# Four raw weight tiles of one part each in the place of two tiles of two parts

## The chip, the cores and the metric

The kernel runs on one core of a Trainium2 chip. A time is the device time of one execution in microseconds (us). The five engines of the core are named as the profile names them: PE (TensorE, matmuls and transposes; PEld are its weight loads), ACT (ScalarE), DVE (VectorE), POOL (GpSimd) and SP (SyncE, which here issues the weight and input transfers; SPq is its queue). Each engine works through its own instructions in order and waits on semaphores for the others.

## The reference

Two layers of a decoder trunk on 256 tokens of 1024 features, in float32. All weights come from device memory; each is used once.

```
def rmsnorm(x, g):  y = x * rsqrt(mean(x * x) + EPS);  return y * g
def swiglu(x, w_gate, w_up, w_down):  return (silu(x @ w_gate) * (x @ w_up)) @ w_down     # d_ff = 2752

per layer:
    h = h + 0.5 * swiglu(rmsnorm(h, ffn1_norm), ffn1 weights)
    u = rmsnorm(h, mix_norm);  z = u @ w_in                    # one projection, cut into columns:
        # mLSTM q|k (short causal convolution, SiLU), v, output gate, input and forget gates,
        # attention q, k, v, and two merge gates gm, ga
    A = sigmoid(o) * head_rmsnorm(mlstm_chunkwise(q, k, v, i, f), m_out_norm)
    B = sliding_window_attention(qknorm(q), qknorm(k), v, sinks)            # window 128
    h = h + (sigmoid(gm) * (A @ w_branch_m) + sigmoid(ga) * (B @ w_branch_a)) @ w_out
    h = h + 0.5 * swiglu(rmsnorm(h, ffn2_norm), ffn2 weights)
    h = h + sigmoid(rmsnorm(h, ple_norm) @ ple_gate_w) * (p[i] @ ple_proj_w)
return h
```

## The kernel before

The 256 tokens are two tiles of 128 (t = 0 and 1). The residual h stays on chip as two tiles of 128 tokens by 1024 features. A block (FFN, mixer, embedding gate) begins with a norm of each token tile: ACT sums squares (`sq`), DVE makes the mean (`ms`), POOL the power -1/2 (`r`), DVE the normed tile (`xn`), PE transposes it (`tp`), and ACT and DVE write the transpose in two pieces (`uT`).

Every product is made of three matmuls on split operands: a float32 value is cut into a rounded high piece (made by ACT, a cast) and the rest (made by DVE, a subtract), and high x high, high x low and low x high are summed. So each weight passes through three steps. SP loads a raw float32 tile (`raw`); ACT casts it to `wh`; DVE subtracts and writes `wl`. The unit of this is a *part*: 1024 columns over 128 partitions, 512 KB. Split parts live in a ring of eight pairs of tiles (RING = 8); a part leaves the ring when PE's last matmul on it is done. A raw tile holds two parts, 1 MB, and there are two raw tiles (RAW = 2). A raw tile is free for the next load when the subtract of its second part is done.

The order of all instructions is fixed when the kernel is built. A planner (class Clock) keeps an assumed time for each engine; every instruction that is written adds its assumed cost. `tick`, which is called between groups of matmuls, lets chains that are due (norms, transposes, splits, the tails of blocks) write their next step, and then calls `feed`, which starts the split of the next part if a ring place is free, its raw tile has arrived by the planner's time, and ACT and DVE are at most AHEAD ahead of PE. What is not due yet is forced by `need`, just before the matmuls that use it. The arrival of a raw tile is planned by `Clock.load`: after the tile is free and the loads before it are through, 2.9 us per MB, and a latency, `DMA = (1.0, 2.9)`. `prefetch` writes a load as soon as a raw tile is free, in the order of the list `pending`, which `unit`, `pair`, `halves`, `columns` and `ffn` fill when the blocks are set up.

The loads all go through SP's one queue: raw tiles (line 324), gains of the norms (`g`, line 498, broadcast to 128 partitions), and the embedding input `p` (line 720). At the start SP loads the first gain row, the two halves of h for t = 0, the first raw tile in two halves, h for t = 1, and the second raw tile. In the FFN, the gate and up products are `pg` and `pu` (the first columns and the last ones are `gu`), the down product `dn`; the mixer's projections are `kvq` (attention k, v, q), `v`, `og`, `z`, `gt`; `ya` and `ym` are the branch products, `yo` the output product. In the embedding gate, `pp` is the product of p and `pg` that of the gate; DVE multiplies them (`sg<-sg,pp`) and adds to h, once for each token tile and each half of the features.

Nearly all engine instructions are written through one helper, so they carry line 130.

Of the kernel before, what the change touches and what calls it, by code (L numbers as in the profile page):

```python
# [11 lines left out]
F32 = mybir.dt.float32  # L12
# [15 lines left out]
HU, QU = 2048, 1024  # L28
# [5 lines left out]
RAW = 2  # L34
# [15 lines left out]
class Part:  # L50


    def __init__(self, c0, k, n):
        self.c0, self.k, self.n = c0, k, n
        self.hi = self.lo = self.ready = None
        self.fresh = True
        self.rows = None


class Clock:  # L60
# [8 lines left out]
    DMA = (1.0, 2.9)  # L69
# [94 lines left out]
class Trunk:  # L164
# [127 lines left out]
    def unit(self, w, c0, n=NB):  # L292

        src = w[:, c0 : c0 + n].rearrange("(k p) n -> p k n", p=P)
        k = min(KT, HU // n)
        return sum((self.columns(src[:, i : i + k, :]) for i in range(0, KT, k)), [])
# [4 lines left out]
    def halves(self, src):  # L301

        units = [[], []]
        for h in range(2):
            for u in range(2):
                units[u] += self.load([Part(i * QU, 2, NB) for i in range(2)], *src(u, h))
        return units

    def pair_halves(self, w, c0):
        rows = lambda h: w[h * (D // 2) : (h + 1) * (D // 2), :].rearrange("(k p) n -> p k n", p=P)  # L310
        view = lambda raw: raw.rearrange("p (k n) -> p k n", k=KT // 2)
        return self.halves(lambda u, h: [(view, rows(h)[:, :, c0 + u * NB : c0 + (u + 1) * NB])])

    def prefetch(self, n=RAW, cut=False):

        while self.pending and self.raws and len(self.loaded) < n:
            parts, copies = self.pending.popleft()
            raw = self.rawp.tile([P, HU], F32, tag="raw", name=self.name("raw"))
            ready, arrivals = self.raws.popleft(), []
            for i in range(1 + cut):  # L320
                for view, src in copies:
                    k = src.shape[1]
                    ks = slice(i * k // 2, (i + 1) * k // 2) if cut else slice(0, k)
                    self.nc.sync.dma_start(view(raw)[:, ks], src[:, ks])
                arrivals.append(self.clock.load(ready, 1.0 / (1 + cut)))
            self.loaded.append((raw, deque((part, arrivals[i if cut else 0]) for i, part in enumerate(parts))))

    def feed(self, must=False):
# [4 lines left out]
        raw, parts = self.loaded[0]  # L333
        part, arrival = parts[0]
# [7 lines left out]
        parts.popleft()  # L342
        last = not parts
        if last:
            self.loaded.popleft()
# [4 lines left out]
        def chain():  # L350
            src = raw[:, part.c0 : part.c0 + w]
# [222 lines left out]
    def ffn(self, xT, wg, wu, wd, sink, first=6):  # L574
# [48 lines left out]
        def last_features(c0):  # L623

            def half(i):
                return lambda raw: raw[:, : KT * P].rearrange("p (k n) -> p k n", k=KT)[:, :, i * rest : (i + 1) * rest]
            unit = self.load([Part(0, KT, P)], *[(half(i), w[:, c0:].rearrange("(k p) n -> p k n", p=P))
                                                 for i, w in enumerate((wg, wu))])
# [11 lines left out]
        for k0 in range(0, nk - 2, 2):  # L640
            down += self.columns(wd[k0 * P : (k0 + 2) * P, :].rearrange("(k p) n -> p k n", p=P))
        down += self.load([Part(i * D, 1, D) for i in range(2)],
                          (lambda raw: raw[:, :D], wd[(nk - 2) * P : (nk - 1) * P, :]),
                          *[(lambda raw, p=p: raw[p, D:], wd[(nk - 1) * P :, :]) for p in (low, high)])
# [81 lines left out]
    def mix(self, l, xT, sink):  # L726
# [63 lines left out]
        rows = lambda g: lambda raw: raw[g * AD : (g + 1) * AD, :].rearrange("p (k n) -> p k n", k=4)  # L790
        units_a = self.halves(lambda u, h: [(rows(g), wa[g, :, h, :, half(u)]) for g in range(2)])
# [54 lines left out]
    def run(self, stages=None):  # L846
# [19 lines left out]
        with self.tc.manual_schedule(engines={EngineType.PE, EngineType.Activation, EngineType.DVE, EngineType.SP}):  # L866
# [4 lines left out]
            self.prefetch(1, True)  # L871
# [410 lines left out]
```

## Time and profile before

| | us |
|---|---|
| three runs | 1392.11, 1394.45, 1393.32 (median 1393.32) |
| the profiled execution, whole | 1395.02 |
| its span, first to last instruction | 1393.2 |
| PE busy, matmuls | 1371.4 (98%) |
| DVE busy | 862.3 (62%) |
| ACT busy | 726.7 (52%) |
| POOL busy | 55.0 (4%) |
| DMA, mean | 175 GB/s, 243.81 MB |

The page lists busy time of each engine, the chain of work that ended last, the costliest groups and the transfers. A row of the timeline has the start, the length, the engine, the program's line, the operation, what it writes and reads, and in brackets how long the engine sat idle before it and what ended that. A row of the waits has the engine and operation that waited, what it waited for, the total in us, how often, and the longest. "Issue to landing" of a transfer is from its instruction on SP to its completion.

### The profile page before, as it was taken

Reading aid. Unit: us, or ns where it says so; the run is one execution under the profiler, and the core shown is the slowest. Engines: PE = TensorE matmul, PEld = TensorE weight load, DVE = VectorE, ACT = ScalarE, POOL = GpSimd, SP = SyncE. Lnnn points to the kernel's source line nnn. Section 1 sums busy time; section 2 is a strip of 40 time slices with the busy share of each in tenths; the row PEclk is TensorE's granted clock in tenths of the full one; section 3 lists DMA queues with packets and bytes.
Section 4 is the critical chain, followed back from the end, with each engine's and each line's share of the span. In section 5 each row is a group of like instructions: output and inputs, shape, how many; then the busy total and the mean of one; then the engine's idle time right before and its main releaser. Section 6 shows DMA issues by size and latency. Waiting matters only on the chain.

```text
span 1393.2 us, 21942 instructions
## 1 busy us (share of the span) xinstructions
PE 1371.4 (98%) x9056; PEld 1236.9 (89%) x9056; DVE 862.3 (62%) x1213; ACT 726.7 (52%) x1138; POOL 55.0 (4%) x84
## 2 busy tenths in 40 slices
PE   8999999999999999999999999999999999999998
PEld 5999887899899889988779998878998998999886
DVE  5655457765886665554575554586658876555544
ACT  5555346874665454443554443477756554544433
POOL 0000012000000000000000000120000000000000
PEclk9999999999999999999999999999999999999999
DMA  6665645464545565565456566455445554655551
GB/s 209 218 210 167 228 136 196 124 149 151 168 152 182 166 212 186 169 229 182 165 164 210 172 207 208 143 164 145 135 134 192 173 160 161 227 191 170 205 181 61
DMA packets 125830, 243.81 MB, mean 175 GB/s; under 512 B 14977, under 2 KB 23841, under 8 KB 125730
## 3 DMA queue, kind: packets, MB, share of 16 engines
q1 hardware_dynamic: 125730, 242.41, 54.6%
q8 instruction: 71, 1.16, 0.4%
q14 instruction: 29, 0.24, 0.0%
HBM read 241.34 MB, written 1.05 MB: 174 GB/s over the span
## 4 chain that ended last, share of the span: by engine, by line
PE 90%; DMA 3%; DVE 3%; ACT 2%; issue 1%; POOL 0%; SPq 0%; ACTq 0%; POOLq 0%
PE dn L130 16%; PE pg L130 15%; PE pu L130 14%; PE gu L130 7%; PE z L130 7%; PE gt L130 6%; PE ya L130 4%; PE ym L130 3%; PE v L130 3%; PE og L130 3%; PE yo L130 3%; PE kvq L130 3%; PE tp L130 2%; PE sc L130 1%; DVE wl L130 1%; PE ha L130 1%
## 5 line engine op out<-in xcount | busy, mean ns | idle before, releaser
L130 DVE TENSOR_TENSOR wl<-raw,wh 128x1024 fp32r<-128x1024 f32 (+1 forms) x448 | 540.8, 1222 | 365.8 <-ACT wh L130 364.7
L130 ACT CAST wh<-raw 128x1024 fp32r<-128x1024 f32 x448 | 461.5, 1050 | 439.8 <-PE dn L130 86.9
L130 PE MATMUL dn<-wh,hid 128*128 128x512 f32 x688 | 218.4, 395 | 0.0
L130 PE MATMUL pg<-uT,wh 128*128 128x256 f32 x1088 | 194.6, 281 | 0.0
L130 PE MATMUL pu<-uT,wh 128*128 128x256 f32 x1088 | 193.6, 281 | 0.0
L130 PEld LDWEIGHTS pg<-uT,wh 128*128 128x128 f32 x1088 | 167.1, 189 | 0.2
L130 PEld LDWEIGHTS pu<-uT,wh 128*128 128x128 f32 x1088 | 166.9, 188 | 0.0
L130 PEld LDWEIGHTS dn<-wh,hid 128*128 128x128 f32 x688 | 129.3, 188 | 29.9
L130 PE MATMUL pg<-uT,wl 128*128 128x256 f32 x544 | 152.9, 281 | 0.0
L130 PE MATMUL pu<-uT,wl 128*128 128x256 f32 x544 | 152.9, 281 | 0.0
L130 PE MATMUL dn<-wl,hid 128*128 128x512 f32 x352 | 138.7, 394 | 0.0
L130 PEld LDWEIGHTS pu<-uT,wl 128*128 128x128 f32 x544 | 102.5, 188 | 0.0
L130 PEld LDWEIGHTS pg<-uT,wl 128*128 128x128 f32 x544 | 102.4, 188 | 0.0
L130 PE MATMUL gt<-uT,wh 128*128 128x256 f32 x512 | 93.2, 283 | 0.0
L130 PE MATMUL z<-uT,wh 128*128 128x256 f32 x512 | 92.1, 282 | 0.0
L130 PE MATMUL gu<-wh,uT 128*128 128x512 f32 x256 | 83.5, 402 | 1.9 <-ACT uT L130 1.9
L130 PEld LDWEIGHTS gt<-uT,wh 128*128 128x128 f32 x512 | 79.0, 188 | 1.2
L130 PEld LDWEIGHTS dn<-wl,hid 128*128 128x128 f32 x352 | 66.2, 188 | 15.3
L130 PEld LDWEIGHTS z<-uT,wh 128*128 128x128 f32 x512 | 78.7, 188 | 0.2
L130 PE MATMUL z<-uT,wl 128*128 128x256 f32 x256 | 72.0, 281 | 0.0
L130 PE MATMUL gt<-uT,wl 128*128 128x256 f32 x256 | 71.9, 281 | 0.0
L130 PE MATMUL kvq<-wh,uT 128*128 128x512 f32 x192 | 63.7, 401 | 0.0
(194 smaller groups left out, 2034.2 us busy)
## 6 DMA issues: line engine op xcount, KB each, us to landing
raw<-in_w_in_dram SPq DMA_DIRECT2D x60, 1024.0 KB, 5.1
raw<-in_ffn_w_up_dram SPq DMA_DIRECT2D x40, 1024.0 KB, 5.2
raw<-in_ffn_w_down_dram SPq DMA_DIRECT2D x40, 1024.0 KB, 5.5
raw<-in_ffn_w_gate_dram SPq DMA_DIRECT2D x39, 1024.0 KB, 5.7
raw<-in_w_branch_a_dram SPq DMA_DIRECT2D x16, 512.0 KB, 5.9
raw<-in_w_branch_m_dram SPq DMA_DIRECT2D x8, 1024.0 KB, 5.1
raw<-in_w_out_dram SPq DMA_DIRECT2D x8, 1024.0 KB, 5.1
raw<-in_ple_gate_w_dram SPq DMA_DIRECT2D x8, 1024.0 KB, 7.3
```

The costliest lines, as they stand in the source:

```text
L130: return issue(*args, **kw)
```

## The change

A raw tile now holds one part (1024 columns, 512 KB), and there are four of them; together they take the same space as before. A tile is free as soon as the subtract of its one part is done. Each part is its own transfer: SP's rows rise from 292 instructions to 513 in the whole program. The planner reckons with a latency of 2.0 us instead of 1.0, so that a part is planned to arrive 0.5 x 2.9 + 2.0 = 3.45 us after its load can start, where a pair was planned to take 2.9 + 1.0 = 3.9. The first loads are the same: the first raw tile was already loaded in two halves.

```diff
-HU, QU = 2048, 1024
+QU = 1024
...
-RAW = 2
+RAW = 4
...
-    DMA = (1.0, 2.9)
+    DMA = (2.0, 2.9)
...
-    def load(self, parts, *copies):
-
-        self.pending.append((parts, copies))
-        return parts
-
-    def columns(self, src, p=None):
+    def part(self, k, n, *copies):
+
+        self.pending.append(Part(k, n, copies))
+        return self.pending[-1]
+
+    def columns(self, src):
 
         _, k, n = src.shape
-        run = QU // n
-        view = lambda raw: raw[:, : k * n].rearrange("p (k n) -> p k n", k=k)
-        return self.load([Part(i * n, min(run, k - i), n) for i in range(0, k, run)], (view, src))
+        run = min(k, QU // n)
+        view = lambda raw: raw[:, : run * n].rearrange("p (k n) -> p k n", k=run)
+        return [self.part(run, n, (view, src[:, i : i + run, :])) for i in range(0, k, run)]
...
-    def prefetch(self, n=RAW, cut=False):
+    def prefetch(self, n=RAW):
 
         while self.pending and self.raws and len(self.loaded) < n:
-            parts, copies = self.pending.popleft()
-            raw = self.rawp.tile([P, HU], F32, tag="raw", name=self.name("raw"))
-            ready, arrivals = self.raws.popleft(), []
-            for i in range(1 + cut):
-                for view, src in copies:
-                    k = src.shape[1]
-                    ks = slice(i * k // 2, (i + 1) * k // 2) if cut else slice(0, k)
-                    self.nc.sync.dma_start(view(raw)[:, ks], src[:, ks])
-                arrivals.append(self.clock.load(ready, 1.0 / (1 + cut)))
-            self.loaded.append((raw, deque((part, arrivals[i if cut else 0]) for i, part in enumerate(parts))))
+            part = self.pending.popleft()
+            raw = self.rawp.tile([P, QU], F32, tag="raw", name=self.name("raw"))
+            for view, src in part.copies:
+                self.nc.sync.dma_start(view(raw), src)
+            self.loaded.append((raw, part, self.clock.load(self.raws.popleft(), 0.5)))
...
         self.store += 1
         ready = max(self.free.popleft(), arrival)
-        parts.popleft()
-        last = not parts
-        if last:
-            self.loaded.popleft()
+        self.loaded.popleft()
...
             part.ready = clock.done()
-            if last:
-                self.raws.append(part.ready)
-                self.prefetch()
+            self.raws.append(part.ready)
+            self.prefetch()
...
-            self.prefetch(1, True)
+            self.prefetch(2)
```

`halves`, `pair_halves`, `unit`, the last columns of the FFN and its down weights are written anew in the same sense: one part, one load.

No engine's compute instructions change in number or kind. Because the planned arrivals and the times at which raw tiles come free differ, their order does: 504 of PE's 9096 positions, 187 on ACT and 324 on DVE. Three places follow; a name like `wl_293` is a tile with its number in the program.

DVE at the start of the program, from the subtract of the second part on. `xn_3..` is the norm of t = 1, `uT_114` and `uT_115` its transposed low pieces, `wl` are splits. Before:

```order
L130 TENSOR_TENSOR wl_254<-raw_230,wh_253 128x1024
L130 SCALAR_TENSOR_TENSOR ms_288<-ss_270 128x1
L130 SCALAR_TENSOR_TENSOR xn_301<-h_89,r_289,g_224 128x512
L130 SCALAR_TENSOR_TENSOR xn_303<-h_89,r_289,g_225 128x512
L130 TENSOR_TENSOR wl_293<-raw_234,wh_292 128x1024
L130 TENSOR_TENSOR uT_114<-tp_309,uT_112 128x4x128
L130 TENSOR_TENSOR uT_115<-tp_316,uT_113 128x4x128
L130 TENSOR_TENSOR wl_299<-raw_234,wh_298 128x1024
```

Now:

```order
L130 TENSOR_TENSOR wl_259<-raw_232,wh_258 128x1024
L130 SCALAR_TENSOR_TENSOR ms_296<-ss_275 128x1
L130 TENSOR_TENSOR wl_291<-raw_235,wh_290 128x1024
L130 SCALAR_TENSOR_TENSOR xn_315<-h_89,r_297,g_224 128x512
L130 SCALAR_TENSOR_TENSOR xn_317<-h_89,r_297,g_225 128x512
L130 TENSOR_TENSOR wl_304<-raw_237,wh_303 128x1024
L130 TENSOR_TENSOR wl_310<-raw_256,wh_309 128x1024
L130 TENSOR_TENSOR uT_114<-tp_328,uT_112 128x4x128
L130 TENSOR_TENSOR uT_115<-tp_335,uT_113 128x4x128
```

The third part's subtract stands before the norm instead of behind it, and those of the fourth and fifth part stand before `uT`. On PE all six matmuls of the third part for t = 0 now come before the transposes of t = 1, where three came after them.

DVE at the end of the first layer's embedding gate, from the first `sg<-sg,pp` of t = 0 on; `h_88` is the residual of t = 0, `h_89` that of t = 1, the last `xn` the norm of t = 0 for the next layer. Before:

```order
L130 SCALAR_TENSOR_TENSOR sg_6988<-sg_6988,pp_6904 128x512
L130 SCALAR_TENSOR_TENSOR h_88<-sg_6988,h_88 128x512
L130 TENSOR_TENSOR wl_6983<-raw_6942,wh_6982 128x1024
L130 TENSOR_TENSOR wl_7007<-raw_6942,wh_7006 128x1024
L130 TENSOR_TENSOR wl_7013<-raw_6968,wh_7012 128x1024
L130 SCALAR_TENSOR_TENSOR sg_7031<-sg_7031,pp_6904 128x512
L130 SCALAR_TENSOR_TENSOR h_88<-sg_7031,h_88 128x512
L130 SCALAR_TENSOR_TENSOR ms_7037<-ss_6992 128x1
L130 SCALAR_TENSOR_TENSOR sg_7047<-sg_7047,pp_6907 128x512
L130 SCALAR_TENSOR_TENSOR h_89<-sg_7047,h_89 128x512
L130 SCALAR_TENSOR_TENSOR xn_7064<-h_88,r_7038,g_6853 128x512
```

Now:

```order
L130 TENSOR_TENSOR wl_7191<-raw_7130,wh_7190 128x1024
L130 TENSOR_TENSOR wl_7209<-raw_7166,wh_7208 128x1024
L130 SCALAR_TENSOR_TENSOR sg_7220<-sg_7220,pp_7123 128x512
L130 SCALAR_TENSOR_TENSOR h_88<-sg_7220,h_88 128x512
L130 TENSOR_TENSOR wl_7232<-raw_7178,wh_7231 128x1024
L130 SCALAR_TENSOR_TENSOR sg_7258<-sg_7258,pp_7123 128x512
L130 SCALAR_TENSOR_TENSOR h_88<-sg_7258,h_88 128x512
L130 SCALAR_TENSOR_TENSOR ms_7264<-ss_7224 128x1
L130 SCALAR_TENSOR_TENSOR sg_7274<-sg_7274,pp_7126 128x512
L130 SCALAR_TENSOR_TENSOR h_89<-sg_7274,h_89 128x512
L130 SCALAR_TENSOR_TENSOR xn_7291<-h_88,r_7265,g_7070 128x512
```

Between the two `sg` of t = 0 stands one split where there were three; two splits moved ahead of the first `sg`. On ACT likewise, one cast stands between the same two steps where there were two.

SP near the end of the first layer's second FFN: the raw tiles of the down weights, the gain of the embedding norm and `p`. Before:

```order
L324 DMA raw_6287<-in_ffn_w_down_dram 128x2x1024
L324 DMA raw_6342<-in_ffn_w_down_dram 128x2x1024
L324 DMA raw_6402<-in_ffn_w_down_dram 128x2x1024
L498 DMA g_6437<-in_ple_norm_dram 128x1024
L720 DMA p_6439<-in_p_dram 128x2x256
```

Now:

```order
L319 DMA raw_6550<-in_ffn_w_down_dram 128x1024
L319 DMA raw_6592<-in_ffn_w_down_dram 128x1024
L319 DMA raw_6620<-in_ffn_w_down_dram 128x1024
L487 DMA g_6638<-in_ple_norm_dram 128x1024
L707 DMA p_6640<-in_p_dram 128x2x256
```

`p` comes behind eleven down parts of half a megabyte each, where it came behind ten in five pairs.

In each layer's `kvq` stage one split stands ahead of the first two q norms (`qn`) on DVE, where two stood ahead of all four, and PE's first transposes of them come six matmuls earlier.

More of the change, by code (lines that the diff above doesn't have):

```diff
@@ L50, with __init__ @@
 class Part:
-    def __init__(self, c0, k, n):
-        self.c0, self.k, self.n = c0, k, n
+    def __init__(self, k, n, copies):
+        self.k, self.n, self.copies = k, n, copies
         self.hi = self.lo = self.ready = None
@@ L277, in consts @@
         mask(self.band[:, P:], 0, -1, 1)
-    def load(self, parts, *copies):
-        self.pending.append((parts, copies))
-        return parts
-    def columns(self, src, p=None):
+    def part(self, k, n, *copies):
+        self.pending.append(Part(k, n, copies))
+        return self.pending[-1]
+    def columns(self, src):
         _, k, n = src.shape
-        run = QU // n
-        view = lambda raw: raw[:, : k * n].rearrange("p (k n) -> p k n", k=k)
-        return self.load([Part(i * n, min(run, k - i), n) for i in range(0, k, run)], (view, src))
+        run = min(k, QU // n)
+        view = lambda raw: raw[:, : run * n].rearrange("p (k n) -> p k n", k=run)
+        return [self.part(run, n, (view, src[:, i : i + run, :])) for i in range(0, k, run)]
     def unit(self, w, c0, n=NB):
-        src = w[:, c0 : c0 + n].rearrange("(k p) n -> p k n", p=P)
-        k = min(KT, HU // n)
-        return sum((self.columns(src[:, i : i + k, :]) for i in range(0, KT, k)), [])
+        return self.columns(w[:, c0 : c0 + n].rearrange("(k p) n -> p k n", p=P))
     def pair(self, w, c0):
@@ L305, in halves @@
             for u in range(2):
-                units[u] += self.load([Part(i * QU, 2, NB) for i in range(2)], *src(u, h))
+                units[u] += [self.part(2, NB, *src(u, k)) for k in (4 * h, 4 * h + 2)]
         return units
     def pair_halves(self, w, c0):
-        rows = lambda h: w[h * (D // 2) : (h + 1) * (D // 2), :].rearrange("(k p) n -> p k n", p=P)
-        view = lambda raw: raw.rearrange("p (k n) -> p k n", k=KT // 2)
-        return self.halves(lambda u, h: [(view, rows(h)[:, :, c0 + u * NB : c0 + (u + 1) * NB])])
-    def prefetch(self, n=RAW, cut=False):
+        w = w.rearrange("(k p) n -> p k n", p=P)
+        view = lambda raw: raw.rearrange("p (k n) -> p k n", k=2)
+        return self.halves(lambda u, k: [(view, w[:, k : k + 2, c0 + u * NB : c0 + (u + 1) * NB])])
+    def prefetch(self, n=RAW):
         while self.pending and self.raws and len(self.loaded) < n:
-            parts, copies = self.pending.popleft()
-            raw = self.rawp.tile([P, HU], F32, tag="raw", name=self.name("raw"))
-            ready, arrivals = self.raws.popleft(), []
-            for i in range(1 + cut):
-                for view, src in copies:
-                    k = src.shape[1]
-                    ks = slice(i * k // 2, (i + 1) * k // 2) if cut else slice(0, k)
-                    self.nc.sync.dma_start(view(raw)[:, ks], src[:, ks])
-                arrivals.append(self.clock.load(ready, 1.0 / (1 + cut)))
-            self.loaded.append((raw, deque((part, arrivals[i if cut else 0]) for i, part in enumerate(parts))))
+            part = self.pending.popleft()
[3 more added lines that the diff above has]
+            self.loaded.append((raw, part, self.clock.load(self.raws.popleft(), 0.5)))
     def feed(self, must=False):
@@ L332, in feed @@
             return
-        raw, parts = self.loaded[0]
-        part, arrival = parts[0]
+        raw, part, arrival = self.loaded[0]
         slack = AHEAD[self.store >= STORE]
@@ L350, in chain @@
         def chain():
-            src = raw[:, part.c0 : part.c0 + w]
+            src = raw[:, :w]
             if part.rows is None:
@@ L626, in half @@
                 return lambda raw: raw[:, : KT * P].rearrange("p (k n) -> p k n", k=KT)[:, :, i * rest : (i + 1) * rest]
-            unit = self.load([Part(0, KT, P)], *[(half(i), w[:, c0:].rearrange("(k p) n -> p k n", p=P))
-                                                 for i, w in enumerate((wg, wu))])
+            unit = [self.part(KT, P, *[(half(i), w[:, c0:].rearrange("(k p) n -> p k n", p=P))
+                                       for i, w in enumerate((wg, wu))])]
             def run():
@@ L639, in ffn @@
         down = []
[L640 to L644, printed above, removed]
+        for k in range(nk - 1):
+            down.append(self.part(1, D, (lambda raw: raw, wd[k * P : (k + 1) * P, :])))
+        down.append(self.part(1, D, *[(lambda raw, p=p: raw[p], wd[(nk - 1) * P :, :]) for p in (low, high)]))
         down[-1].rows = low
@@ L789, in mix @@
         wa = a["w_branch_a"][l].rearrange("(b g j d) n -> g d b j n", b=2, g=2, j=4)
-        rows = lambda g: lambda raw: raw[g * AD : (g + 1) * AD, :].rearrange("p (k n) -> p k n", k=4)
-        units_a = self.halves(lambda u, h: [(rows(g), wa[g, :, h, :, half(u)]) for g in range(2)])
+        rows = lambda g: lambda raw: raw[g * AD : (g + 1) * AD, :].rearrange("p (k n) -> p k n", k=2)
+        units_a = self.halves(lambda u, k: [(rows(g), wa[g, :, k // 4, k % 4 : k % 4 + 2, half(u)]) for g in range(2)])
         def use_a(k, ps):
```

## The prediction

> **What bounds the kernel now.** I read the page first (busy times, the chain that ended last), then the span, then the waits of each engine (engine and what it waited for: us in total, times, longest).
>
> ```profile
> PE 1371.4 (98%) x9056; PEld 1236.9 (89%) x9056; DVE 862.3 (62%) x1213; ACT 726.7 (52%) x1138; POOL 55.0 (4%) x84
> ...
> PE 90%; DMA 3%; DVE 3%; ACT 2%; issue 1%; POOL 0%; SPq 0%; ACTq 0%; POOLq 0%
> ```
>
> ```profile
> core 0: 1393.2 us, clock 0.997
> ```
>
> TensorE (PE) works 98% of the span and holds 90% of the chain that ended last; the mean granted clock is 0.997. All that can be won without touching the matmuls is PE's idle time, 1393.2 - 1371.4 = 21.8 us, plus what a lowered clock costs. PE's waits say who holds it:
>
> ```profile
> PE tp L130 <- DVE xn L130: 3.9, 2, 2.6
> PE ya L130 <- DVE qT L130: 2.7, 2, 1.3
> ...
> PE gu L130 <- DVE wl L130: 1.5, 2, 0.8
> ```
>
> Split weights hold PE directly twice, 1.5 us. The other engines do wait for raw weights:
>
> ```profile
> ACT wh L130 <- DMA raw<-in_ffn_w_down_dram: 56.6, 24, 6.2
> ...
> SPq L324 <- DVE wl L130: 1016.9, 208, 15.2
> ```
>
> ACT waits long for arrivals, and the DMA queue (SPq) stands 1016.9 us behind the subtracts that free raw buffers. The ring of eight split tiles hides nearly all of it. So the change can act only at a few places where a norm or transpose that PE needs stands behind a split in an in-order queue, or a small load behind a big one.
>
> **The steady stages: 0.** The rows are windows (start:end and length, busy us of PE, PEld, DVE, ACT and POOL, granted clock, DMA share, GB/s), then groups and DMA issues of the page.
>
> ```profile
> 40.00:400.00 360.00, 357.72 (x2428) 323.63 (x2427) 230.02 (x350) 203.40 (x353) 17.94 (x24) 1.00 0.56 175
> ...
> 15.09:18.50 3.41, 2.75 (x16) 2.04 (x15) 1.75 (x2) 0.77 (x2) 0.00 (x0) 1.00 0.84 291
> ```
>
> ```profile
> L130 DVE TENSOR_TENSOR wl<-raw,wh 128x1024 fp32r<-128x1024 f32 (+1 forms) x448 | 540.8, 1222 | 365.8 <-ACT wh L130 364.7
> L130 ACT CAST wh<-raw 128x1024 fp32r<-128x1024 f32 x448 | 461.5, 1050 | 439.8 <-PE dn L130 86.9
> ...
> raw<-in_ffn_w_gate_dram SPq DMA_DIRECT2D x39, 1024.0 KB, 5.7
> ...
> raw<-in_ffn_w_gate_dram SPq DMA_DIRECT2D x6, 512.0 KB, 4.0
> ```
>
> In the long window PE is busy 357.72 of 360 us and the DMA engines 0.56. PE uses 448 parts in 1393 us, one per 3.1 us. Before, a raw buffer is bound for 5.7 + 1.05 + 2 x 1.22 = 9.2 us per two parts; with two buffers, 2.3 us per part. After, 4.0 + 1.05 + 1.22 = 6.3 us per part with four buffers, 1.6 us. If the four share the 291 GB/s of the fastest stretch, 0.52 MB takes 1.8 us, four 7.2 us, a buffer's cycle 9.5 us, and a part 2.4 us: still under 3.1. Both versions supply more than PE takes, so I cost the added overlap at nothing; the ring hides it. SP's issues about double, 221 more, each 0.37 us in the rows at 675.67 and 1295.71 below, take 82 us, inside its 1016.9 us of waiting. The same arithmetic instructions run.
>
> The Trainium skill, "DMA: Bandwidth & Descriptors", section "Bandwidth", speaks against the change: it asks for at least 1 MiB per DMA. The rows agree that a small transfer is dear (half the bytes, 4.0 of 5.7 us); by the rule the stages would turn DMA-bound only if transfers did not overlap, which is a rival below.
>
> **From the embedding gate to the next layer's FFN, near 675 to 699: -2.0.**
>
> ```profile
> 674.53 0.34 SPq L498 DMA_DIRECT2D g<-in_ffn_norm_dram  x1
> ...
> 675.67 0.37 SPq L324 DMA_DIRECT2D raw<-in_ple_gate_w_dram  x1
> ...
> 691.76 1.05 ACT L130 CAST wh<-raw 128x1024 fp32r<-128x1024 f32 x1 [1.28 <-DMA raw<-in_ffn_w_gate_dram]
> ...
> 692.84 1.22 DVE L130 TENSOR_TENSOR wl<-raw,wh 128x1024 fp32r<-128x1024 f32 x1 [1.11 <-ACT wh L130]
> ...
> 693.98 0.68 DVE L130 SCALAR_TENSOR_TENSOR sg<-sg,pp 128x512 f32<-128x512 f32 x1
> ...
> 695.43 0.63 ACT L130 ACTIVATE sq<-h 128x512 f32<-128x512 f32 x1 [2.13 <-DVE h L130]
> ...
> 696.06 0.58 ACT L130 ACTIVATE sg<-pg 128x512 f32<-128x512 f32 x1
> ...
> 698.00 1.41 DVE L130 SCALAR_TENSOR_TENSOR xn<-h,r,g 128x512 f32<-128x512 f32 x2
> ...
> 698.81 1.32 PE L130 MATMUL tp<-ident,xn 128*128 128x128 f32 x8 [2.58 <-DVE xn L130]
> ```
>
> The rows are the timeline (start, length, engine, what it writes and reads, and in brackets the idle time before and what ended it). Read backwards: PE waits for xn, which stands behind sg and h of the second token tile, behind sq, behind the DVE's sg at 693.98, which stands behind a subtract whose cast waited 1.28 us for its transfer. In the new order one split stands between the two sg of this chain where two stood on ACT and three on DVE. The transfer is freed one subtract earlier, too: a raw buffer no longer waits for its second part. Its queue holds the gain g at 674.53 and a raw tile behind it at 675.67; what follows g there needs 0.5 MB, not 1 MB, before it can be used, so these loads should land 1.5 to 2.5 us sooner, so ACT reaches the last cast near 689 instead of 691.76. Then the subtract ends by 691.3, sg by 692.0, h by 692.7, sq by 693.4, the second tile's sg and h by 695.4, xn starts 2.6 us earlier, and PE's wait is gone. If the transfer lands as late as now, the subtract ahead of sg ends as late and nothing is won. Bounds 0 and -2.6; I take -2.0, nearer the large end because two causes are removed together. The stall then goes to the split behind it: the next gu waits 0.8 us for a wl already, and may keep it.
>
> **The p load in each layer: -1.4.**
>
> ```profile
> 1295.71 0.37 SPq L324 DMA_DIRECT2D raw<-in_ffn_w_down_dram  x1
> ...
> 1296.68 0.38 SPq L720 DMA_DIRECT2D p<-in_p_dram  x1
> ...
> 1303.03 0.63 PE L130 MATMUL tp<-ident,p 128*128 128x128 f32 x4 [1.68 <-DMA p<-in_p_dram]
> ...
> 612.75 0.63 PE L130 MATMUL tp<-ident,p 128*128 128x128 f32 x4 [0.40 <-DMA p<-in_p_dram]
> ```
>
> p lands 6.3 us after its issue, behind a raw tile of 1 MB issued 1 us ahead, which is then 0.5 MB. From the 1 MB and 512 KB rows that is 5.7 - 4.0 = 1.7 us less to move. But p's issue moves behind one more down part; freed by its own subtract, not by a pair's, I put it 0.3 to 0.8 us later. Net -0.9 to -1.4 each, capped by PE's waits 0.40 and 1.68: -0.4 and -1.0. Bounds -2.1 and, with nothing won in transit, +1.6 (twice the later issue).
>
> **The q norm in the second layer: -0.2.**
>
> ```profile
> 914.77 4.00 POOL L130 TENSOR_TENSOR r<-s,mhalf 128x8 f32<-128x8 f32 x2 [10.19 <-DVE s L130]
> ...
> 916.06 2.37 DVE L130 TENSOR_TENSOR wl<-raw,wh 128x1024 fp32r<-128x1024 f32 x2 [0.57 <-ACT wh L130]
> ...
> 918.35 1.40 DVE L130 TENSOR_TENSOR qn<-kvq,r 128x256 f32<-128x256 f32 x4
> ...
> 919.14 0.66 PE L130 MATMUL tp<-ident,qn 128*128 128x128 f32 x4 [0.57 <-DVE qn L130]
> ```
>
> One subtract instead of two now stands ahead of qn (1.2 us sooner), but PE asks for it six 512-wide matmuls, near 1.4 us, sooner, and the first r ends near 914.77 + 4.00/2 = 916.8, so two qn of 0.35 each end near 917.5, and PE asks near 919.14 - 0.57 - 1.4 = 917.2. That leaves a wait of 0.3 to 0.4 of the 0.57; in the first layer, where the same place had no wait, I expect none. Bounds -0.6 and +1.2 (0.6 late in both layers).
>
> **Start-up: 0.**
>
> ```profile
> 14.30 1.41 DVE L130 SCALAR_TENSOR_TENSOR xn<-h,r,g 128x512 f32<-128x512 f32 x2 [0.67 <-POOL r L130]
> ...
> 15.62 1.22 DVE L130 TENSOR_TENSOR wl<-raw,wh 128x1024 fp32r<-128x1024 f32 x1
> ...
> 16.90 0.50 PE L130 MATMUL gu<-wl,uT 128*128 128x512 f32 x1 [0.66 <-DVE wl L130]
> ...
> 18.72 1.29 DVE L130 TENSOR_TENSOR uT<-tp,uT 128x512 fp32r<-128x512 f32 x2 [1.88 <-ACT uT L130]
> ```
>
> The third part's subtract now precedes xn, which wins the 0.66 us at 16.90. Two more subtracts now precede the second token tile's uT, which can then start near 15.7 + 1.4 + 2 x 1.22 = 19.5 instead of 18.72, a loss of 0.8: behind them on DVE stand that uT and the splits after it, and PE's first product of the second tile waits for it. The split of the up part that stands there needs a transfer issued only when the very first subtract is done, and 4.0 us long. Bounds -0.7 and +1.5 (the extra split's transfer late).
>
> **The attention branch: 0.**
>
> ```profile
> 321.25 0.39 PE L130 MATMUL ya<-qT,wh 128*128 128x256 f32 x1 [1.34 <-DVE qT L130]
> ```
>
> ```profile
> 318.88:322.29 3.41, 1.79 (x15) 1.40 (x15) 1.91 (x3) 2.08 (x3) 0.00 (x0) 1.00 0.59 186
> 322.29:325.70 3.41, 3.41 (x18) 3.41 (x17) 0.00 (x0) 0.88 (x3) 0.00 (x0) 0.50 0.76 286
> 694.34:697.75 3.41, 1.89 (x9) 1.19 (x7) 2.23 (x5) 1.21 (x3) 0.55 (x1) 1.00 0.57 220
> ...
> 1011.78:1015.20 3.42, 3.42 (x18) 3.25 (x16) 0.00 (x0) 0.91 (x4) 0.00 (x0) 0.50 0.69 267
> ```
>
> The order around qT is the same, so its wait stays. After a stretch with PE busy 1.79 of 3.41 us the clock was 0.50 for 3.41 us, costing about 1.7; after one with 1.89 it was not. Such a drop hangs on where idle time falls. The second layer has one too, at 1011.78. As the idle time moves a little in every stage, the drops can vanish (-3.4) or a third can come (+1.7); I take no change.
>
> The Trainium skill, "TensorE: Matmul & The Clock Gate", Part 1, has a free-running window of 3413 ns, which fits these stretches. By it the same stalls may cost 1.7 us or nothing from run to run.
>
> **Sum.** -2.0 - 1.4 - 0.2 = -3.6 us against the profiled execution's 1395.02 (span 1393.2 and 1.8 around it): 1391.4. That execution lies 1.7 us above the median of the three runs, 1393.32; on that median the forecast is 1389.7.
>
> **Rivals.** *Nothing measurable:* weights hold PE for 1.5 us only, and a stall removed reappears at the next chain: 1393, against it the two late transfers above. *Slower:* a split is queued ahead of a norm chain and its transfer, or its own 1.22 us, makes PE wait. Places: uT at start-up and qn in both layers, 1.22 each = 3.7, with nothing won at 698: 1397. It decides if the chain's split is cast later than its predecessor was before; for it speaks that PE asks for qn earlier. *Larger gain:* all of 2.6, 2.1, 0.7 and one clock drop of 1.7: 7.1, so 1386.2. *Not what it says:* if transfers of 4.0 us came one after another, 448 of them would take 1792 us, about 1790; against it stand 291 GB/s in the fastest stretch, over twice what one 0.52 MB in 4.0 us makes.
>
> **Numbers.** Forecast 0.48, nothing 0.22, slower 0.15, larger gain 0.12, DMA-bound 0.03. This kernel's measurement tells about 0.2%, 2.8 us, from no change. The forecast's own range, 1387.8 to 1391.8, lies seven tenths below 1390.5; with the larger gain that makes faster 0.46, same 0.36, slower 0.18. The range 1385.5 to 1396.0 takes in the larger gain and most of the slower case.
>
> **What would show it.** In the new profile tp<-xn near 698 should wait under 1 us, tp<-p at most 0.7 in the second layer, the long FFN stretches should keep PE above 99%, and 512 KB loads should land in 4 to 6 us. A wait of tp<-qn, or of gu<-uT at start-up, over 1 us would speak for the slower rival; median landings over 9 us for the DMA-bound one; an unchanged 2.6 us for nothing won.

## The result, and the profile after

The changed kernel takes 1397.55 us (median of six executions, 1395.89 to 1400.61), the kernel before, run beside it, 1392.37 us (1391.37 to 1394.45): a ratio of 1.0036, interval 1.0023 to 1.0049. It became slower by about 5 us where I had forecast 3.6 us faster. Run again beside the first experiments, it gave 1.0038 (1.0026 to 1.0050).

The profiled execution took 1398.03 us with a span of 1396.2, 3.0 more than before. From the page after (span, busy times):

```profile
span 1396.2 us, 22582 instructions
...
PE 1374.3 (98%) x9056; PEld 1238.2 (89%) x9056; DVE 867.0 (62%) x1213; ACT 730.0 (52%) x1138; POOL 55.5 (4%) x84
```

The waits of PE after:

```profile
PE sc L130 <- ACT pr L130: 3.5, 4, 1.0
PE gt L130 <- DVE qT L130: 2.9, 2, 1.4
PE ya L130 <- DVE qT L130: 2.7, 2, 1.3
...
PE tp L130 <- DVE xn L130: 2.2, 2, 1.4
PE gu L130 <- DVE wl L130: 0.8, 1, 0.8
...
PE tp L130 <- DMA p<-in_p_dram: 0.5, 1, 0.5
```

The first two rows are new: PE waits 3.5 us for the exponentials of the attention scores (`pr`) and 2.9 us for `qT`, both in the attention stage. What I had looked at became better: xn from 3.9 to 2.2 us, p from 2.1 to 0.5, and the wait for the q norms is no longer there. The long FFN stretches, in the windows, are full, as they were before:

```profile
30.00:200.00 170.00, 170.00 (x1154) 156.42 (x1153) 91.14 (x94) 74.95 (x90) 3.29 (x4) 1.00 0.65 192
345.00:600.00 255.00, 255.00 (x1885) 241.87 (x1884) 173.07 (x259) 134.25 (x189) 6.29 (x10) 1.00 0.60 180
```

To see where the difference lies I summed, from the trace, what PE loses in each stage: for every matmul the distance from the start of the one before, less the shortest regular distance of its form (118 ns for 256 columns, 232 for 512, 109 for 128). Half-clock stretches are contained in it. In us, for profiled executions:

| stage (us of the span) | before | after | difference |
|---|---|---|---|
| start (0 to 30) | 5.9 | 4.8 | -1.2 |
| mixer, layer 1 (200 to 345) | 5.9 | 10.3 | +4.4 |
| second FFN's end, embedding gate, layer 1 (600 to 720) | 4.7 | 2.8 | -1.9 |
| mixer, layer 2 (885 to 1040) | 6.9 | 9.5 | +2.6 |
| p, layer 2 (1285 to 1320) | 1.9 | 0.0 | -1.9 |
| all the rest | 1.4 | 1.8 | +0.4 |
| sum | 26.7 | 29.1 | +2.4 |

Outside the mixer the change gains 5.0 us in three rows of the table, 1.2 of it at the start, where the prediction had 0 and where I don't count it below; the mixer takes 7.0 back. The differences add up to 2.4 us, and the spans differ by 3.0: 0.6 us is not in the sum, and a mixer's row can shift by up to 0.5 us with the distance that one takes as regular for the attention's small matmuls. How the mixer takes its 7 us is seen in the timeline near 234 to 243. Rows of before (ACT's square of the last q product, its table load, the first exp; PE's third score block):

```profile
236.88 0.60 ACT L130 ACTIVATE sq<-kvq 128x512 f32<-128x512 f32 x1 [1.93 <-PE kvq L130]
...
237.49 1.28 ACT L130 ACT_TABLE_LOAD   x1
...
238.79 0.37 ACT L130 ACTIVATE pr<-sc,mx 128x128 f32<-128x128 f32 x1
...
243.05 0.61 PE L130 MATMUL sc<-band,identb 128*128 128x512 bf16 x2
```

and of after, from the second score block on:

```profile
235.06 0.97 PE L130 MATMUL sc<-kT,qT 64*128 64x256 f32 x12
...
237.66 0.60 ACT L130 ACTIVATE sq<-kvq 128x512 f32<-128x512 f32 x1 [2.28 <-PE kvq L130]
...
238.28 1.28 ACT L130 ACT_TABLE_LOAD   x1
...
239.57 0.37 ACT L130 ACTIVATE pr<-sc,mx 128x128 f32<-128x128 f32 x1
...
241.13 0.38 PE L130 MATMUL sc<-band,identb 128*128 128x512 bf16 x1 [0.72 <-ACT pr L130]
...
241.99 0.40 ACT L130 ACTIVATE pr<-sc,mx 128x128 f32<-128x128 f32 x1
...
242.53 0.38 PE L130 MATMUL sc<-band,identb 128*128 128x512 bf16 x1 [1.02 <-ACT pr L130]
```

In the new order the q norms are transposed earlier and the score blocks follow earlier, so that six matmuls of the last q products now come after the second score block (none before; in both orders three more stand between the first block and the second). In ACT's queue the square of the last product stands ahead of the exps: it waits for PE until 237.66, the table load follows it, and the eight exps of the first score block come behind both, at 239.57. PE meanwhile has only 18 matmuls between the second and the third score block, where it had 21, and then stands: its first matmul there starts when four exps are done, the second when all eight are. In the built program these eight exps read banks 1 and 3 of the accumulators, and the third block is given the same banks 1 and 3; before, the first block held 1 and 0 and the third was given 1 and 6, and it started when the exps were long done.

The second new wait, in the same stage:

```profile
282.44 1.09 PE L130 MATMUL tp<-ident,pr 128*128 128x128 f32 x8
282.55 0.69 DVE L130 TENSOR_REDUCE mx<-sc 128x2 f32<-128x512 f32 x1 [0.47 <-PE sc L130]
...
284.14 0.68 DVE L130 TENSOR_TENSOR qT<-ha,qT 128x512 fp32r<-128x512 f32 x1
...
284.98 0.47 PE L130 MATMUL gt<-uT,wh 128*128 128x256 f32 x2 [1.44 <-DVE qT L130]
```

Eight transposes of pr now follow a score block at once; before, 18 gate matmuls came between the block and the first four of them, and qT was written meanwhile, at 282.05. What makes PE wait is again a bank. In the built program the product `ha` that qT is made from lies in bank 2, and the gate product `gt` behind the transposes is given bank 2 too, so that it can't start before DVE's qT has read ha. In DVE's queue qT stands behind the two reductions of the score block (`mx`, from 282.55), and is done at 284.8. Before, ha lay in bank 3, and the gt behind the score block went to banks 2 and 4. The second layer is alike: bank 6 for both in the change.

The wait at 241 to 243 was followed by a stretch at half clock, in the windows of after:

```profile
240.40:243.80 3.40, 1.66 (x15) 0.86 (x13) 1.91 (x7) 3.40 (x16) 1.74 (x9) 0.97 0.00 0
243.80:246.80 3.00, 3.00 (x10) 2.30 (x9) 2.40 (x5) 1.45 (x7) 0.00 (x0) 0.50 0.29 53
```

The clock records of the traces show such stretches, each of 3.41 us; one costs PE 1.4 to 1.6 us by the measure of the table. The change has three (at 243.58, 325.5 and 1015.0), before has two (at 322.29 and 1011.78), behind the waits of ya.

### The profile page after: what moved, and what is told of

It is laid out like the page before. It is cut to its first block, busy times and chain, and to the rows that moved or that the text cites. A ratio compares the mean times of both kernels' runs of the same rounds, so it can differ in the third digit from the quotient of the medians.

```text
span 1396.2 us, 22582 instructions
## 1 busy us (share of the span) xinstructions
PE 1374.3 (98%) x9056; PEld 1238.2 (89%) x9056; DVE 867.0 (62%) x1213; ACT 730.0 (52%) x1138; POOL 55.5 (4%) x84
## 5 line engine op out<-in xcount | busy, mean ns | idle before, releaser
L130 ACT CAST wh<-raw 128x1024 fp32r<-128x1024 f32 x448 | 467.3, 1050 | 432.9 <-PE dn L130 111.9
```

Source lines behind the costliest of these rows:

```text
L130: return issue(*args, **kw)
```

## The experiments

The change has two parts, the tiles with their loads and releases, and the order that the planner makes of them. The order of PE, ACT and DVE can be held apart from the tiles, since it is fixed when the kernel is built. My first theory was that the order alone makes the loss; the rival, that twice as many, smaller transfers cost the time. All ratios are to the kernel before, run beside.

**e1: new tiles, order of before.**

```diff
+        self.groups, self.empty = deque(), RAW        # planner: pairs, as before; loads: single parts
+    def fetch(self, n=RAW):
+        while self.pending and self.empty and n:
+            part = self.pending.popleft()
+            part.raw = self.rawp.tile([P, QU], F32, tag="raw", name=self.name("raw"))
...
+            self.empty += 1
+            self.fetch()
+            if last:
+                self.raws.append(part.ready)
+                self.prefetch()
```

> Four raw tiles of one part, loads as in the change, but the planner keeps the arrivals and releases of two tiles of two parts and a latency of 1.0: on PE, ACT and DVE the order is that of before, instruction for instruction. Order theory (the loss is the new order in the attention stage, 3.7 + 1.1 us in the first layer and 2.2 + 0.9 in the second, and the tiles themselves help): no wait of PE for pr at the second score block, no wait of 1.4 us of gt for qT, the p wait in the second layer gone or under 0.7 us (before 1.84), the start about 1 us shorter, in all 2 to 4 us faster than before, near 0.998. Tile theory (twice as many, smaller transfers cost the time): about 5 us slower, near 1.0036, as the change.

Measured: 1393.3 us beside 1392.33, 1.0008 (1.0000 to 1.0017). Neither theory's number. The attention waits are not there, as the order theory says, and the transfers are not to blame for 5 us. But the gain of 2 to 4 us was not there either. In the profile PE lost 1.4 us from 600 to 720, where before lost 4.7: the xn wait of 2.6 us near 699 and the first layer's p wait are gone, from the tiles alone. At the second layer's p it lost 4.8 where before lost 1.9:

```profile
1293.06 0.39 SPq L730 DMA_DIRECT2D p<-in_p_dram  x1
...
1300.84 0.67 PE L130 MATMUL tp<-ident,p 128*128 128x128 f32 x4 [3.02 <-DMA p<-in_p_dram]
```

p took 7.8 us from issue to use here, and 1.6 us of half clock followed. Two raw tiles of half the size were issued at 1291.04 and 1292.17, within 2.0 us ahead of it, as many bytes as the one tile of 1 MB that stands 1.0 us ahead of p in before, where p took 6.3. In the first layer of e1 only one raw tile was issued in the 4 us ahead of p, and p was there when PE asked. What else made it late in the second layer is open.

**e2: tiles of before, order of the change.**

```diff
-        self.free, self.raws = deque([0.0] * RING), deque([0.0] * RAW)
+        self.free, self.raws = deque([0.0] * RING), deque([0.0] * 4)      # planner: four single parts
+        self.empty, self.planned = RAW, deque()                           # loads: two pairs
```

> Two raw tiles of two parts, loads as before, but the planner reckons with four tiles of one part and a latency of 2.0: on PE, ACT and DVE the order is that of the change. Order theory: the attention waits of the change are all there (PE waits for pr near 241 and 932, gt for qT near 285 and 975), the gains of the tiles at the start and at p are not, the gain near 699 in part: 5 to 8 us slower than before, 1.004 to 1.006. Tile theory: no slower than before within 0.1%.

Measured: 1438.3 us, 1.0342 (1.0324 to 1.0360): the sign that the order theory gave, and a size that no theory gave. PE's waits:

```profile
PE tp L130 <- DVE sg L130: 8.7, 5, 2.8
PE gu L130 <- ACT uT L130: 5.8, 3, 2.1
PE if L130 <- DVE wif L130: 5.5, 2, 2.8
PE tp L130 <- DVE xn L130: 4.1, 2, 2.7
PE sc L130 <- ACT pr L130: 4.0, 5, 1.0
```

None of these is a wait for a split weight. About 17 of the 46 us is half clock behind the waits: eleven stretches, where before has two. The new order puts casts into ACT's queue at the times at which single parts would have come; with pairs they come later, ACT and DVE stand at them, and what is queued behind (sg, uT, wif, xn) is late. One such place, near 520 to 528:

```profile
521.20 2.00 ACT L130 CAST wh<-raw 128x1024 fp32r<-128x1024 f32 x2 [2.58 <-DMA raw<-in_ffn_w_up_dram]
...
525.22 1.99 ACT L130 CAST wh<-raw 128x1024 fp32r<-128x1024 f32 x2 [2.02 <-DMA raw<-in_ffn_w_up_dram]
526.30 1.23 DVE L130 TENSOR_TENSOR wl<-raw,wh 128x1024 fp32r<-128x1024 f32 x1 [1.65 <-ACT wh L130]
527.44 1.28 DVE L130 TENSOR_TENSOR sg<-sg,gu 128x512 f32<-128x512 f32 x2
528.17 1.25 PE L130 MATMUL tp<-ident,sg 128*128 128x128 f32 x8 [2.75 <-DVE sg L130]
```

So tiles and order are not two costs that add: this order is dear with tiles for which it was not planned.

**e3: the change, and the planner may do other work between the exps of one score block and the matmuls of the next.** Without this point the planner writes the next block as soon as it has written the exps, whenever they will be done.

```diff
         for j0 in range(0, 4, per):
+            if j0:
+                yield
             js = slice(j0, j0 + per)
```

> The change, with one more point in the scores chain at which the planner may go on with other work: between the exps of one score block and the matmuls of the next. The next block is then written when the exps are planned to be done (27 v matmuls and more after the block before, in the place of 18). If PE's waits for pr are the exps that hold the score banks, they vanish in both layers and the half-clock stretch after the first goes too: 5 to 7 us faster than the change, near 1391, or 0.999 of before. If the waits come from late splits or transfers, they stay, and so does the time, 1.0036.

Measured: 1388.06 us, 0.9967 (0.9955 to 0.9979), faster than both kernels: 9.5 us below the change, where I had expected 5 to 7. No wait for pr or of gt is left; the mixers lose 4.4 and 4.6 us where the change lost 10.3 and 9.5. What stands there now:

```profile
PE if L130 <- DVE wif L130: 3.0, 2, 1.5
...
PE tp L130 <- DVE xn L130: 1.6, 2, 1.3
PE gu L130 <- DVE wl L130: 0.8, 1, 0.8
PE ya L130 <- DVE qT L130: 0.7, 2, 0.3
```

The edit moves about 180 instructions of PE against the change (by a line comparison of the two built orders), and the third block is given banks 3 and 6, where the first held 1 and 3. So it is not the wait for pr alone that it removes: the gt wait (2.9 us) and most of the ya wait (2.7 to 0.7) went too, and a wait for wif came.

**e4: the change again.**

> The change once more, beside the others on one chip: 1.0036 of before, between 1.0023 and 1.0049, with PE's four waits for pr (3.5 us) and two of gt for qT (2.9 us).

Measured: 1397.58 us, 1.0038 (1.0026 to 1.0050), with the same rows, 3.5 us for pr and 2.9 for qT.

**e5: the extra point alone, in the kernel before.** The edit is that of e3.

> The kernel before with the same extra point in the scores chain, raw tiles and latency untouched. If the extra point alone makes the third experiment's gain, this is 0.997 of before. If the gain needs the new tiles too, this is between 0.999 and 1.001: before, PE had no wait for pr in the first score blocks, only two of 0.6 us near 285 and 975.

Measured: 1405.24 us beside 1391.57, 1.0098 (1.0084 to 1.0112). The extra point is no gain in itself, and neither of the two outcomes that I had named came. (The two waits of before near 285 and 975 that I had put down to pr are for `ptd`, 0.45 and 0.47 us.) With it the planner puts the last score blocks so late that the attention's end finds no cover; PE waits for the transposed probabilities (`ptd`), four times in each layer, and more than 3 us in each:

```profile
PE ha L130 <- DVE ptd L130: 7.0, 8, 1.6
```

**e6 and e7: each half of the change alone.**

```diff
-    DMA = (2.0, 2.9)        # e6, in the change
+    DMA = (1.0, 2.9)
...
-    DMA = (1.0, 2.9)        # e7, in the kernel before
+    DMA = (2.0, 2.9)
```

> The change with its planned latency put back to 1.0, tiles as changed; half of the change alone. Now 21 v matmuls stand between the two score blocks where the change has 18 (and before 21), 0.7 us more cover, but the transposes of pr still follow a score block at once. Order theory: PE waits for pr near 1.3 us per layer instead of 2.1, gt's wait of 1.4 for qT stays, in all 1.001 to 1.003 of before. If the longer latency alone was the cause: 0.998 of before.

Measured: 1390.69 us, 0.9995 (0.9986 to 1.0004). No wait for pr, none of gt; ya waits longer, 4.9 us in all. Both are against my expectation of waits of 1.3 and 1.4 us, and the rows show why (the 21 matmuls of the expectation are three of the last q product and 18 of v):

```profile
238.66 0.60 ACT L130 ACTIVATE sq<-kvq 128x512 f32<-128x512 f32 x1 [4.41 <-PE kvq L130]
...
239.28 1.28 ACT L130 ACT_TABLE_LOAD   x1
...
242.63 0.60 PE L130 MATMUL sc<-band,identb 128*128 128x512 bf16 x2
242.64 0.39 ACT L130 ACTIVATE pr<-sc,mx 128x128 f32<-128x128 f32 x1
...
242.98 0.40 ACT L130 ACTIVATE pr<-sc,mx 128x128 f32<-128x128 f32 x1
```

The square of the last q product is ahead of the exps here too, and they begin at 240.57, later than in the change. Yet the third block starts at 242.63 without a wait, while two exps of the first block still run. In the built program the first block holds banks 1 and 6 and the third is given 1 and 3; the four exps that read bank 1 were done at 242.0, and the two that still run read bank 6. So late exps alone don't make PE wait: the next block must also be given the banks that they read. Likewise gt: ha lies in bank 3, and gt goes to 7, 6 and 5.

> The kernel before with the planned latency 2.0 and nothing else; the other half of the change alone. The order moves at 375 places of PE, and again the transposes of pr follow a score block at once. Order theory: slower by 1 to 6 us, 1.001 to 1.004, with waits of PE for pr or of gt for qT. If the latency is harmless: 0.999 to 1.001.

Measured: 1391.32 us, 0.9994 (0.9985 to 1.0003). One wait of 0.5 us for pr (the third block is given the first block's banks, 1 and 0, and its second matmul waits), one of 0.7 of gt, and a new one of 3.3 us of the `if` product for wif. Against my expectation neither half is slower: of these three kernels only the one with both halves has the order with the 3.5 and 2.9 us of waits.

**e8: e3 with the latency at 1.0.**

> The third experiment (new tiles, extra point in the scores) with the planned latency at 1.0. If the tiles and the extra point make the gain and the latency does nothing, as the third: 0.9955 to 0.998 of before. If the longer latency is what lets the new tiles gain near 699 and at the q norms, this is slower than the third by 1 to 3 us, 0.998 to 1.000.

Measured: 1398.4 us, 1.0053 (1.0041 to 1.0066), as bad as I had not thought possible for it. The attention's end is late as in e5 (ha waits 5.2 us for ptd, with two half-clock stretches behind it in each layer). The same two edits that made the best kernel so far make a bad one when one planned number differs.

**e9: e3, with the small split of the gate weights written before the gate projection.** PE's order is e3's; many of its products lie in other banks.

```diff
+        self.jobs.append(lambda: setattr(rec, "wif", rec.gate_weights()))
         ga = gate(C_GA)
...
-        w = self.gate_weights()
+        w = self.wif
```

> The third experiment with the split of the gate weights (wif, four small pieces on ACT and DVE) written before the gate projection in the place of after it; PE's order is the third's, instruction for instruction. In the third PE waits 1.5 us in each layer for wif, which stands behind eight scalings of pr on ACT. If that queue is the cause, both waits vanish: 2 to 3 us faster than the third, near 1385.5, 0.995 of before. If another step of the same chain is late as well, the wait passes to it and the time stays at 0.9967.

Measured: 1386.8 us, 0.9965 (0.9952 to 0.9977), the lowest median. The wait for wif is gone, as expected. Of its 3.0 us only 1.3 shows in the medians, and the two intervals are nearly the same, so that e9 and e3, which ran on two different chips, can't be told apart; 1.4 us of new waits for ptd stand earlier in the stage.

**e10: the change with a latency of 2.5.**

> The change with a planned latency of 2.5. Only 12 v matmuls, 2.8 us, stand between the two score blocks, where the change has 18 projection matmuls and the sixth experiment 21; the last kvq product is done before the second block, so that the exps can start earlier against it. If the number of matmuls between the blocks decides, PE waits 1.4 us longer than in the change in each layer, 1.006 of before. If the start of the exps decides (behind sq and the table load, 2.2 us after the last kvq product, and the banks free 3.0 us later), PE waits near 1 us where the change has 2.1: 1.001 to 1.003. The wait of gt for qT (transposes of pr straight after a score block) stays, 1.4 us in each layer, in both cases.

Measured: 1392.34 us, 1.0007 (0.9997 to 1.0016). No wait for pr at all, with only 12 matmuls between the blocks and with the third block in the first block's banks (1 and 7 both times, in the built program). So the number of matmuls does not decide, and the same banks alone do not make a wait. The rows show what else is needed:

```profile
235.61 1.28 ACT L130 ACT_TABLE_LOAD   x1
236.12 0.61 PE L130 MATMUL sc<-band,identb 128*128 128x512 bf16 x2
...
236.90 0.37 ACT L130 ACTIVATE pr<-sc,mx 128x128 f32<-128x128 f32 x1
...
239.32 0.40 ACT L130 ACTIVATE pr<-sc,mx 128x128 f32<-128x128 f32 x1
239.66 0.64 ACT L130 ACTIVATE sq<-kvq 128x512 f32<-128x512 f32 x1
...
240.44 0.60 PE L130 MATMUL sc<-band,identb 128*128 128x512 bf16 x2
```

Here the square of the last q product stands behind the eight exps in ACT's queue, not ahead of them. They begin at 236.90, while PE is still at the second block, and are done at 239.7; PE comes at 240.44 and finds the banks free. With e6 this gives the condition from both sides: PE waits where the exps are late and the third block is given a bank that they still read; e6 lacks the second, e10 the first. The wait of gt, 2.9 us, is there as expected, with bank 0 for ha and for the gt behind the transposes in the first layer.

**e11: the change, first score blocks held until the last q product is written.**

```diff
+                while (2, NT - 1) not in self.inputs:
+                    yield
```

> The change with the first score blocks held until the last kvq product is written, so that no sq stands before the exps waiting for PE. Between the second block and the third stand 27 matmuls. No wait of PE for pr at the third block in either layer (2.1 us each in the change); the wait of gt for qT stays, as the transposes of pr follow a score block at once there too: 3 to 5 us faster than the change, 0.9995 to 1.002 of before. If the waits for pr are not the bulk of the change's loss: 1.003 and more.

Measured: 1388.68 us, 0.9976 (0.9967 to 0.9984). The wait for pr is gone, as expected, and the time fell by more than that: gt does not wait either, though transposes of pr follow a score block at once in this order too; ya waits 0.7 instead of 2.7, while wif costs 3.9. That a score block and eight transposes in a row make gt wait holds in the change and in e10 and not here, so that pattern alone is not its cause. The banks tell the orders apart: here ha lies in bank 7 and gt goes to 0 and 5, and qT stands ahead of the reductions in DVE's queue, done at 282.1, before they begin at 282.85. In the built programs gt waits 1.4 us in each layer of the change, e2 and e10 with ha and gt in one bank, and does not in before, e6 and e11 with two.

All kernels with what PE lost in the profiled execution (us, as in the first table; values of some tenths, and the one below zero, are within the error of the measure):

| | start | mixer 1 | 600 to 720 | mixer 2 | p, layer 2 | rest | ratio |
|---|---|---|---|---|---|---|---|
| before | 5.9 | 5.9 | 4.7 | 6.9 | 1.9 | 1.4 | 1 |
| the change | 4.8 | 10.3 | 2.8 | 9.5 | 0.0 | 1.8 | 1.0036 |
| the change again (e4) | 5.5 | 7.6 | 2.4 | 9.4 | 0.2 | 1.9 | 1.0038 |
| new tiles, old order (e1) | 6.0 | 5.6 | 1.4 | 6.3 | 4.8 | 1.7 | 1.0008 |
| old tiles, new order (e2) | 9.1 | 17.5 | -0.2 | 16.5 | 0.2 | 25.9 | 1.0342 |
| e3 | 6.6 | 4.4 | 2.1 | 4.6 | 0.3 | 2.7 | 0.9967 |
| e5 | 5.9 | 9.9 | 4.2 | 10.4 | 2.1 | 2.9 | 1.0098 |
| e6 | 6.1 | 5.5 | 1.7 | 5.9 | 0.8 | 2.3 | 0.9995 |
| e7 | 5.8 | 4.5 | 4.4 | 5.6 | 0.1 | 3.2 | 0.9994 |
| e8 | 6.6 | 9.2 | 1.9 | 9.5 | 1.2 | 2.3 | 1.0053 |
| e9 | 4.4 | 3.4 | 2.2 | 3.9 | 0.4 | 3.9 | 0.9965 |
| e10 | 5.0 | 7.8 | 1.7 | 8.2 | 0.2 | 1.5 | 1.0007 |
| e11 | 6.2 | 6.0 | 2.2 | 6.2 | 0.0 | 1.3 | 0.9976 |

With new tiles and an order planned for them (the change, e3, e6, e8 to e11) the 600 to 720 stretch loses 1.7 to 2.8 us and p in the second layer 0.0 to 1.2; those gains are steady. What sets these kernels apart is the mixers: 7.3 us in both layers together for e9, 9.0 for e3, 11.4 for e6, 12.2 for e11, 16.0 for e10, 18.7 for e8, 17.0 to 19.8 for the change. That is nearly the order of their times too; e11 is faster than e6 against it. Part of it is the clock, about 1.5 us for each stretch at half clock: e3, e7 and e9 have none in the mixers, before, e6, e10 and e11 two, the change three and, run again, one, and e8 four.

## Why the prediction was wrong, step by step

- **Steady stages 0:** right. PE is busy 170.00 of 170 us and 255.00 of 255 us in the FFN stretches after. That both versions supply more than PE takes was true, but as a mean: e2 shows that an order written for releases by part starves with tiles released by pair. That a surplus of supply hides a late part holds only if nothing that PE needs is queued behind that part.
- **Embedding gate -2.0:** right. PE's stall at the transposes of xn went from 2.74 to 0.98 us, -1.8. From PE's last matmul ahead of them to the first of the transposes 2.16 us pass in before and 0.41 after: xn is there 1.8 us sooner against PE. The wait behind it, 0.8 us of gu for a wl, stayed, as the step said. e1, where the order is that of before, shows that the tiles make this gain.
- **p -1.4:** right in sum, not in its parts. First layer 0.57 to 0.62, nothing won where 0.4 was forecast: p was issued 0.7 us later against PE and landed 0.6 us sooner after its issue. Second layer 1.84 to 0, where 0.7 should have been left: p was there when PE asked, at most 5.0 us after its issue (6.3 before). e1's 7.8 us, with smaller tiles ahead of p and as many bytes close ahead, shows that smaller tiles do not make it sure.
- **q norm -0.2:** too small; the wait of 0.73 us is gone. The two r took 3.24 us here, not 4.00, and began 1.2 us sooner, so that qn was written at 916.36 and PE did not ask before 919.
- **Start-up 0:** -1.2 in the profile of the change, because the first cast could begin at 6.72 us, not 8.25. In e3, with the same loads, PE's first product is at 11.16, as before, so I do not count that as a gain of the change. The term stays unsettled between 0 and -1.2. The two splits ahead of uT cost PE nothing: DVE was idle for 0.3 us before uT, waiting for ACT.
- **Attention branch 0: this step failed.** It held the order around qT of `ya` for the whole attention stage. That wait did stay (2.7 us in both). But PE's order had moved at hundreds of places (504 by the count put on record; a line comparison of the built orders gives 240 to 370), and most of the stage's were not read for the prediction: the q norms' transposes, three score blocks, the transposes of pr. With 3.5 us for pr, 2.9 for qT at gt, and the half-clock stretch after the first, the mixers lost 7.0 us more, the 0.7 won at qn already taken off. Both waits are for an accumulator bank that another engine still reads, ACT's late exps in the one and DVE's late qT in the other; that the banks of PE's products move with the order was not looked at either.
- **The slower rival** had the size (1397, which the range, up to 1396.0, did not take in) and not the place. It had a weight split ahead of a norm chain, at uT and qn. No weight split makes the new waits: an attention square ahead of the exps in ACT's queue does, with a score block that PE reaches soon and that is given the banks of those exps. As that rival said, PE was late where it asks earlier for a chain; it was the score block and not qn.
- **DMA-bound:** refuted by the full FFN stretches. The 1 MiB rule of the Trainium skill, "DMA: Bandwidth & Descriptors", section "Bandwidth", did not bear on the time: e1 doubles the loads and halves them in size, with the same order, for 1.0008 (1.0000 to 1.0017). How long a split load takes to land is not on the page of the changed kernel, so that check of the prediction could not be made.
- **The median against the profile.** The profiled executions differ by 3.0 us, the medians by 5.2. The profile of before lies 2.7 us above its median, at a mean clock of 0.997, and holds about 3 us of half clock behind the two ya waits. That other executions of before have fewer such stretches fits what stands on record beside the experiments: in 61 more executions of that kernel the middle time was 1390.4 us at a mean clock of 1.000, 1392.0 at 0.999, 1392.6 at 0.998, 1392.8 at 0.997 and near 1395 below. Of the changed kernel's six the shortest has the highest mean clock (1395.89 us at 0.998); the others lie at 0.995 to 0.997. In the two profiles of the change the half-clock stretches fell differently: behind the pr wait in the first (10.3 us lost in mixer 1), not in the second (7.6).

## What to carry to other kernels

Where a planner writes the order, a change of buffers or of a planned latency is above all a new order. Read the moved rows of every engine in the stages in which PE waits for chains of other engines (here scores, exps, transposes), and ask at each what PE reaches sooner and what is ahead of it in the other engine's queue; a mean of supply and demand answers neither. Judge the tiles and the order apart by building each with the other's, and give the order the point at which it could have waited (here between exps and the next score block), then measure again, since the same edit can lose with another order (0.9967 in e3, 1.0098 in e5). Ask also which accumulator bank PE's next product is given and who still reads it: in both new waits of this change that was what held PE, and a kernel with exps as late (e6) had no wait because its banks had fallen otherwise.

## What the runs showed that I had not expected

- An order of the same instructions, planned for four single tiles and run with two pairs, costs 46 us (1.0342); planned and run alike, neither the tiles nor the order came near that.
- Half clock came after stretches that were not idle: PE was busy 1.67 of 3.41 us before the one at 243.58 in the change. The Trainium skill, "TensorE: Matmul & The Clock Gate", Part 1, lets the clock fall after an idle window; here a window half busy was enough, and by the prediction's row at 694.34 one 1.89 of 3.41 us busy was not. No busy share divides the two: in e2 the clock fell after windows 1.90, 1.94 and 1.96 of 3.41 us busy. What decides stays open.
- One planned number, 1.0, 2.0 or 2.5 us, with the same tiles gave 0.9995, 1.0036 and 1.0007, not in order of its size; with the extra point, 1.0 gave 1.0053 and 2.0 gave 0.9967.
